# Projections of an attention layer in chunks of 512 columns instead of 256, with weights in three places and transposes dealt out one token tile behind

## The chip, the cores and the metric

The kernel runs on one core of one Trainium2 chip. The metric is the device time of one execution in microseconds (us), lower is better. The engines are named as in the profile: PE (TensorE, matrix products and transposes), PEld (its weight loads), DVE (VectorE), ACT (ScalarE), POOL (GpSimd) and SP (SyncE, which here only issues DMAs). They run at the same time, each its own instructions in order, and wait for each other by semaphores.

## The reference, cut to what matters

One inference step of a two-layer decoder. The first layer is a matrix LSTM, the second is attention with forget gates; each is followed by a SwiGLU feed-forward part. A prompt of 16 + 1024 tokens and a sample batch of 8 x 8 tokens use the same weights, so T = 1104 token rows are worked on. The change lies in the second mixer, in these projections (D = 1024, 16 heads of 64 columns):

```python
def shared_kv(h, g_kv, w_kvf, b_f, k_g):
    xs = rmsnorm(h, g_kv)
    p = xs @ w_kvf
    k = rmsnorm(p[..., :HD].reshape(B, T, H_B, DH_B), k_g)
    v = p[..., HD:2 * HD].reshape(B, T, H_B, DH_B)
    lf = jax.nn.log_sigmoid((p[..., 2 * HD:] + b_f).astype(jnp.float32))
...
    q = rmsnorm(p[..., :HD].reshape(B, T, H_B, DH_B), q_g) * DH_B ** -0.5
    og = p[..., HD:]
    o = attend(q, k, v, lf).reshape(B, T, HD)
    return (o * jax.nn.sigmoid(og)) @ w_out
```

Keys and queries are normalised per head and token row; keys, values and log-forget values are also outputs.

## The kernel before

**Precision.** Every product is made of three fp32r matmuls (`mm3`, L162 to L166): high part by high part, high by low, low by high. Activations and weights are split into a high part (ACT, with the gain of the norm: L228) and a low part (DVE, L229).

**Tokens.** There are nine token tiles `TT`, the first of 80 rows (64 sample, 16 prompt) and eight of 128. Three of them make a group (`GRP`, `TS`: 336, 384 and 384 tokens), held as activation tiles x0, x1 and x2, high and low (x0h, x0l and so on).

**The stage that changes** is the first part of `phase_b` (L1548). It makes the values, keys and queries for all tokens, in chunks of 256 columns: value chunks 3, 1 and 2 (number 3 first, with the 16 forget columns, 272 in all; value columns 0 to 255 were made earlier), then four key chunks and four query chunks. `tm_proj` (L277) does one chunk. It loads the weights as two halves of four blocks of 128 rows (`load_w`, L199: 512 KB each, issued by SP at L221), from ten places of [128, 1088] that were laid out before: two raw, four high, four low, taken in turn. Then for each of the nine token tiles it does 8 blocks x 3 = 24 matmuls into one PSUM bank (`tmps`, four of them), with the token tile as the loaded operand and the weights as the moving one. `evac` empties the bank.

- For values, `evac` is one copy on ACT into `vst`; the rows go out by POOL's DMA queue (`out_p_v` and the scratch `vD`, 1 MB each, L1543). After chunk 3 come `forget` (L1699: log-sigmoid on DVE; three groups of transposes `fgps` of the forget columns on PE through one PSUM place, each followed by a copy `ltB` on ACT, L1715; a scan on DVE, transposes `fgcq`), preparation for sample attention, and the loads of the first cache page.
- For keys and queries, `evac` (L1607) copies the bank into `raw` on ACT (L1608), squares it on ACT (L1610), and sums the squares per head on DVE (L1611). After every third token tile `then` (L1643) makes the norms of the group: square root on ACT (L1645), reciprocal on DVE (L1646), and the scaling of `raw` on DVE (128 x 768, L1648).
- `turn` (L1614) transposes a group, one feature block of 128 columns at a time: three PE transposes into `btp` (L1622, two PSUM places), the high part `bhi` on ACT (L1626), the low part `blo` on DVE (L1627, two places each), and POOL's DMA stores into the scratch `kDh`, `kDl`, `qDh`, `qDl` (L1631) and, in the first group, `kS` or `qS` (L1635) from `bst`. For keys POOL also multiplies `raw` by the norm's gain (L1637) and sends the rows out (`out_rows`, L1571). A group's `turn` is put on the list `behind` and is done when the next group's `then` comes, three tiles later.

**Behind the stage.** The output gate's first block is projected (`gate(0)`, L1655 to L1663, `og0ps`), and the last group's turn is done. Then sample attention begins (L1665). It loads the queries `qtS` back from the scratch (L1833), transposes cache pages (`ktp`, L1868, copied to `kT` at L1869) and makes scores (`sps`, L1877); the other gates' matmuls (`bps`) are dealt between. The weights of gate 7 have a place of their own, `w7`.

**What sets the order.** In `phase_b` up to the gate, the order on each engine is chosen by the framework's scheduler from the program order and what is free. In sample attention the order of PE is that of the program text. ACT, DVE and POOL run in the order in which the scheduler emitted them; an instruction that waits holds up all behind it on its engine.

Of the kernel before, what the change touches and what calls it, by code (L numbers as in the profile page):

```python
# [147 lines left out]
class Net:  # L148
# [50 lines left out]
    def load_w(self, pieces, g=None, nk=KT, keep=None):  # L199

        nc = self.nc
        n = sum(p.shape[1] for p in pieces)
        new = lambda pool, nm, dt, bufs: pool.tile([P, max(nk * n, self.wmin)], dt, name=self.uid(nm), tag=nm, bufs=bufs)[
            :, : nk * n].rearrange("p (k n) -> p k n", k=nk)
        if self.slots:

            x = self.slot
            cut = lambda t: t[:, : nk * n].rearrange("p (k n) -> p k n", k=nk)
            raw = cut(self.slots[x % 2])
            self.slot += 1  # L210
        else:
            raw = new(self.wp, "wraw", F32, self.wbufs[0])
        if self.slots and not keep:
            hi, lo = (cut(self.slots[y]) for y in (2 + x % 4, 6 + x % 4))
        else:
            pool, bufs = (keep, 1) if keep else (self.wp, self.wbufs[1])
            hi, lo = (new(pool, nm, F32R, bufs) for nm in ("whi", "wlo"))
        o = 0
        for p in pieces:
            w = p.shape[1]  # L220
            nc.sync.dma_start(raw[:, :, o : o + w], p.rearrange("(k p) n -> p k n", p=P))  # L221
            o += w
        if g is None:
            self.split(raw, hi, lo)
        else:
            for k in range(nk):
                gk = self.gain[:, g + k : g + k + 1]
                nc.scalar.activation(hi[:, k], raw[:, k], AF.Copy, scale=gk)  # L228
# [139 lines left out]
    def mlp(self, H, w, l, heads=None, cb=None):  # L368
# [3 lines left out]
        with self.pool(self.uid("nsp")) as sp, self.pool(self.uid("npp"), bufs=2, space=PSUM) as pn:  # L372
# [3 lines left out]
            if cb:  # L376
# [4 lines left out]
            slots = {x: wp.tile([P, max(self.wmin, KT * P)], F32 if x < 2 else F32R, name=self.uid("slot"))  # L381
                     for x in (range(10) if cb else (*range(2, 10), 0, 1))}
# [1165 lines left out]
def phase_b(self, ys, w7, cb):  # L1548
# [8 lines left out]
    self.lfD = scr("lfD", [NS, HB])  # L1557
    ck = ExitStack()
    sk = ck.enter_context(self.pool("spk"))
    with self.pool("fb", bufs=2) as fp, self.pool("fbp", bufs=2, space=PSUM) as pp:  # L1560
        gn = fp.tile([P, DH], F32, name="gk", bufs=1)
        nc.scalar.dma_start(gn, I["k_norm_b"].partition_broadcast(P))
        gc = fp.tile([P, 2], F32, name="gqk", bufs=1)
# [11 lines left out]
            nc.gpsimd.dma_start(po[NM:, cs].rearrange("(i p) d -> p i d", p=P), t[:, 1:, :])  # L1575

        flat = lambda a: a.rearrange("t h d -> t (h d)")

        for c in (3, 1, 2):
            vs = fp.tile([P, NT, 256], F32, name=f"vst{c}", tag="vst")  # L1580

            def evac(i, m, ps):
                nc.scalar.copy(vs[:m, i, :], ps[:m, :256])
                if c == 3:
                    nc.scalar.copy(lf[:m, i, :], ps[:m, 256:272])

            self.tm_proj([wkv[:, D + 256 * c : D + 256 * c + (272 if c == 3 else 256)]], G_KV, pp, "b", 4, evac)
            cs = slice(256 * c, 256 * c + 256)
            self.value_rows(vs, 0, cs)
            if c == 3:  # L1590
                self.forget(lf)
                cq, ncn = self.sample_prep(sk)
                masks = self.sample_masks(sk)
                self.page = {}
                self.load_page(sk, 0)


        behind = []
        for w, g, gi, dst, dstS in ((wkv, G_KV, 0, self.kD, self.kS), (wqo, G_B, 1, self.qD, self.qS)):
            gcol = gc[:, gi : gi + 1]  # L1600
            for c in range(4):
                raw = fp.tile([P, NT, 256], F32, name=self.uid("raw"), tag="raw")
                nc.gpsimd.memset(raw[NS:, 0, :], 0.0)
                ss = fp.tile([P, NT, 4], F32, name=self.uid("ss"), tag="ss")
                nc.gpsimd.memset(ss, 1.0)

                def evac(i, m, ps):  # L1607
                    nc.scalar.copy(raw[:m, i, :], ps[:m, :256])  # L1608
                    sq = fp.tile([P, 256], F32, name=self.uid("sqb"), tag="sqb")
                    nc.scalar.activation(sq[:m], ps[:m, :256], AF.Square)  # L1610
                    nc.vector.tensor_reduce(out=ss[:m, i, :], in_=sq[:m].rearrange("p (h d) -> p h d", d=DH),  # L1611
                                            op=ALU.add, axis=AX.X)

                def turn(q, v4, c=c, raw=raw, gi=gi, gcol=gcol, dst=dst, dstS=dstS):  # L1614
                    for hp in range(2):
                        f = 2 * c + hp
                        ps = pp.tile([P, 512], F32, name=self.uid("btp"), tag="bt")
                        g0, g1 = TS[q]
                        n = g1 - g0
                        for i in GRP[q]:  # L1620
                            t0, t1 = TT[i]
                            nc.tensor.transpose(ps[:, t0 - g0 : t1 - g0], raw[: t1 - t0, i, hp * P : hp * P + P],  # L1622
                                                self.ident[: t1 - t0, : t1 - t0])
                        hi = fp.tile([P, SL], F32R, name=self.uid("bhi"), tag="bhi")
                        lo = fp.tile([P, SL], F32R, name=self.uid("blo"), tag="blo")
                        nc.scalar.activation(hi[:, :n], ps[:, :n], AF.Copy, scale=gcol)  # L1626
                        nc.vector.scalar_tensor_tensor(out=lo[:, :n], in0=ps[:, :n], scalar=gcol,  # L1627
                                                       in1=hi[:, :n].bitcast(F32), op0=ALU.mult, op1=ALU.subtract)
                        o = max(NS - g0, 0)
                        for z, x in enumerate((hi, lo)):  # L1630
                            nc.gpsimd.dma_start(dst[z][f, :, g0 + o - NS : g1 - NS], x[:, o:n].bitcast(F32))  # L1631
                        if q == 0:
                            st = fp.tile([P, T0], F32, name=self.uid("bst"), tag="bst")
                            nc.vector.tensor_scalar(out=st, in0=ps[:, :T0], scalar1=gcol, scalar2=None, op0=ALU.mult)
                            nc.gpsimd.dma_start(dstS[f], st)  # L1635
                    if gi == 0:
                        nc.gpsimd.tensor_tensor(out=v4, in0=v4, in1=gn.unsqueeze(1).broadcast_to([P, 12, DH]),  # L1637
                                                op=ALU.mult)
                    if gi == 0 and q == 2:
                        out_rows(raw, flat(O["p_k"][0]), flat(O["s_k"].rearrange("b t h d -> (b t) h d")),  # L1640
                                 slice(256 * c, 256 * c + 256))

                def then(q, raw=raw, ss=ss, turn=turn):  # L1643
                    qs = slice(3 * q, 3 * q + 3)
                    nc.scalar.activation(ss[:, qs], ss[:, qs], AF.Sqrt, scale=1.0 / DH, bias=self.eps)  # L1645
                    nc.vector.reciprocal(ss[:, qs], ss[:, qs])  # L1646
                    v4 = raw[:, qs, :].rearrange("p i (h d) -> p (i h) d", d=DH)
                    nc.vector.tensor_tensor(out=v4, in0=v4, in1=ss[:, qs, :].rearrange(  # L1648
                        "p i h -> p (i h)").unsqueeze(2).broadcast_to([P, 12, DH]), op=ALU.mult)
                    if behind:  # L1650
                        behind.pop()()
                    behind.append(lambda: turn(q, v4))

                self.tm_proj([w[:, 256 * c : 256 * c + 256]], g, pp, "b", 4, evac, then)
# [715 lines left out]
```

## Time and profile before

| | |
|---|---|
| time, median of 3 runs | 2985.75 us (2976.2 to 2991.02) |
| profiled execution | 2988.03 us |
| its span (first to last instruction) | 2986.3 us |
| mean granted PE clock | 0.984 |
| value chunks 1 and 2, keys and queries | about 1430 to 1682 us |
| one key or query chunk | 27.02 us |

The stage is a twelfth of the span. A row of the timeline gives start, duration, engine, line, operation, output and inputs with shapes, and in brackets the idle time before it with what ended it. Durations of matmuls are modelled ends of a pipelined engine, so that they overlap; the distance from start to start is the pace. "x6" joins six instructions in a row. In a window's row, the columns are busy times of PE, PEld, DVE, ACT and POOL.

### The profile page before, as it was taken

The numbers are of one execution on the slowest core, as the hardware profiler recorded it, in microseconds if no ns is written. First come the engines' busy times: TensorE is split into PE (matmuls) and PEld (weight loads), VectorE is DVE, ScalarE is ACT, GpSimd is POOL, SyncE is SP. The second block draws the span as 40 slices with busy tenths as digits, with TensorE's granted clock in tenths as the row PEclk, the third lists the DMA queues.
The fourth block names the chain that finished last, engine by engine and source line by source line (L and its number), as shares of the span: only waits on it lengthen the run. The fifth ranks groups of instructions, "written<-read, shape, count | busy, mean of one in ns | idle before, by whom it ended". The sixth has DMA issues, their size and how long they took to land.

```text
span 2986.3 us, 52654 instructions
## 1 busy us (share of the span) xinstructions
PE 2881.3 (96%) x20974; PEld 2762.6 (93%) x20974; DVE 1430.3 (48%) x2864; ACT 1140.4 (38%) x2069; POOL 779.4 (26%) x1174
## 2 busy tenths in 40 slices
PE   7999997999999999999999999999999999999999
PEld 7998886999999999999999888777899999999998
DVE  5032456564444455554355543777464444445543
ACT  5122264232222234333344454777332222224432
POOL 2011223313232221104354201454232232231110
PEclk9999799999999999999999999999999999999999
DMA  7052445222222156454354576443413222216653
GB/s 222 7 136 82 114 113 170 94 82 90 72 66 87 54 197 214 155 193 143 128 168 148 196 271 230 159 170 103 139 54 110 74 66 87 71 65 230 210 183 104
DMA packets 298336, 392.73 MB, mean 132 GB/s; under 512 B 31790, under 2 KB 220234, under 8 KB 297066
## 3 DMA queue, kind: packets, MB, share of 16 engines
q1 hardware_dynamic: 260674, 266.90, 27.7%
q0 software_dynamic: 33744, 120.15, 12.2%
q8 instruction: 165, 2.70, 0.4%
q10 hardware_dynamic: 3672, 2.31, 0.3%
q14 instruction: 81, 0.66, 0.1%
HBM read 292.19 MB, written 97.10 MB: 130 GB/s over the span
## 4 chain that ended last, share of the span: by engine, by line
PE 76%; DVE 5%; ACT 3%; issue 3%; POOL 2%; DMA 1%; DVEq 0%; POOLq 0%; ACTq 0%
PE m L1193 21%; PE dps L164 6%; PE dps L166 6%; PE dps L165 6%; PE fps L166 4%; PE fps L164 4%; PE fps L165 4%; PE tmps L164 3%; PE tmps L165 3%; PE tmps L166 3%; PE sp L2157 1%; PE pops L166 1%; PE pops L165 1%; PE pops L164 1%; DVE s L2161 1%
## 5 line engine op out<-in xcount | busy, mean ns | idle before, releaser
L235 DVE TENSOR_TENSOR slot<-slot,slot 128x1024 fp32r<-128x1024 f32 x164 | 207.1, 1266 | 204.4 <-ACT slot L234 204.2
L234 ACT CAST slot<-slot 128x1024 fp32r<-128x1024 f32 x164 | 171.9, 1050 | 336.6 <-PE m L1193 103.3
L166 PE MATMUL fps<-x0h,slot 128*128 128x336 f32 x688 | 219.0, 318 | 1.4 <-DVE slot L235 1.4
L164 PE MATMUL fps<-x0h,slot 128*128 128x336 f32 x688 | 219.4, 319 | 0.1
L165 PE MATMUL fps<-x0l,slot 128*128 128x336 f32 x688 | 218.3, 317 | 0.0
L1193 PE MATMUL m<-x2h,slot 128*128 128x384 f32 x704 | 193.7, 336 | 0.0
L1193 PE MATMUL m<-x1h,slot 128*128 128x384 f32 x672 | 185.9, 338 | 0.0
L307 POOL TENSOR_TENSOR ns<-ns,nq 128x384 f32<-128x384 f32 (+1 forms) x72 | 77.1, 1071 | 278.2 <-ACT nq L305 276.9
L1290 POOL DMA_DIRECT2D hr<-hT x68 | 37.0, 544 | 395.4 <-DMA hT<-fs 84.1
L166 PEld LDWEIGHTS fps<-x0h,slot 128*128 128x128 f32 x688 | 129.8, 189 | 1.9 <-DVE slot L235 1.9
L164 PEld LDWEIGHTS fps<-x0h,slot 128*128 128x128 f32 x688 | 129.9, 189 | 1.3 <-ACT slot L234 0.7
L165 PEld LDWEIGHTS fps<-x0l,slot 128*128 128x128 f32 x688 | 130.1, 189 | 0.4 <-issue 0.3
L1193 PEld LDWEIGHTS m<-x2h,slot 128*128 128x128 f32 x704 | 128.5, 188 | 0.0
L1193 PEld LDWEIGHTS m<-x1h,slot 128*128 128x128 f32 x672 | 123.7, 190 | 0.0
L1193 PE MATMUL m<-x2l,slot 128*128 128x384 f32 x352 | 118.5, 337 | 0.1
L234 ACT CAST slot<-vA 128x1024 fp32r<-128x1024 f32 x53 | 55.5, 1050 | 156.7 <-PE m L1193 76.3
L234 ACT CAST slot<-Ht 128x1024 fp32r<-128x1024 f32 x53 | 55.5, 1049 | 156.1 <-PE m L1193 75.7
L1193 PE MATMUL m<-x1l,slot 128*128 128x384 f32 x336 | 113.4, 337 | 0.0
L235 DVE TENSOR_TENSOR slot<-vA,slot 128x1024 fp32r<-128x1024 f32 x53 | 66.8, 1262 | 85.4 <-ACT slot L234 85.3
L235 DVE TENSOR_TENSOR slot<-Ht,slot 128x1024 fp32r<-128x1024 f32 x53 | 66.9, 1264 | 85.0 <-ACT slot L234 84.9
L2184 ACT ACTIVATE s<-s,nb 128x272 f32<-128x272 f32 (+7 forms) x126 | 98.9, 787 | 0.0
L1193 PE MATMUL m<-T_4h,slot 128*128 128x384 f32 x352 | 97.7, 338 | 0.0
(757 smaller groups left out, 9335.4 us busy)
## 6 DMA issues: line engine op xcount, KB each, us to landing
slot<-in_w_down SPq DMA_DIRECT2D x88, 512.0 KB
fs<-in_w_down SPq DMA_DIRECT2D x44, 512.0 KB
hr<-hT POOLq DMA_DIRECT2D x46, 384.0 KB, 5.2
slot<-in_w_gate_up SPq DMA_DIRECT2D x32, 512.0 KB
kp<-in_cache_k SPq DMA_DIRECT2D x32, 512.0 KB
vp<-in_cache_v SPq DMA_DIRECT2D x32, 512.0 KB
vA<-in_w_gate_up SPq DMA_DIRECT2D x28, 512.0 KB
Ht<-in_w_gate_up SPq DMA_DIRECT2D x28, 512.0 KB
```

The source lines that it names most:

```text
L164: mm(ps, sh, mh, start=first, stop=False)
L165: mm(ps, sh, ml, start=False, stop=False)
L166: mm(ps, sl, mh, start=False, stop=last)
L234: self.nc.scalar.copy(hi, src)
L235: self.nc.vector.tensor_tensor(out=lo, in0=src, in1=hi.bitcast(F32), op=ALU.subtract)
L307: (nc.vector if x == KT - 1 else nc.gpsimd).tensor_tensor(out=s, in0=s, in1=sq, op=ALU.add)
L1193: nc.tensor.matmul(u.ps[b], w[p][:, k], x[q][:, k], start=first and k == i == 0, stop=k == 3 and i == 2, skip_group_check=True)
L1290: nc.gpsimd.dma_start(hraw[j], hT[t][:, 2 * c : 2 * c + 2])
L2157: nc.tensor.matmul(ps[z][:, :n], a[r, qs], b[r, at : at + n], start=(y == 0), stop=(y == 2))
L2161: nc.vector.tensor_tensor_reduce(out=ss[z, u][:, at + o : at + e], in0=ps[z][:, o:e], in1=diag[x][:, z] if y else ncb[:, z, at + o : at + ...
L2184: nc.scalar.activation(ss[z, u], ss[z, u], AF.Exp, bias=nb[:, z : z + 1], accum_out=sm[:, u, z : z + 1])
```

## The change

- **Chunks.** Value chunk 3 with the forget columns stays as it is. The rest is done in five chunks of 512 columns: one of values, two of keys, two of queries (`project`). A token tile is now 24 matmuls of 512 columns into one whole PSUM bank. `raw`, the squares, the sums, the scaling (128 x 1536) and POOL's product (128 x 1536) are twice as wide and half as many. `raw` and `vst` share two places of [128, 9, 512].
- **Weights.** A half chunk is 4 blocks x 512 columns (1 MB), loaded by `load_half`. All half chunks go through one raw place (the two old ones joined). The split parts lie in three places: two from the eight old ones, one in `w7t` (high) and `w3` (low). Half 2x + 2 is asked for at the start of chunk x, half 2x + 3 in its last token tile. The place of gate 7's weights, `w7t`, is therefore laid out ahead of the stage, and `load_w` takes `keep` as a pair of places.
- **Transposes.** A group now has four feature blocks. Each `turn` does one, and two are done behind each token tile's `evac`, from the next tile on: the first two one tile after `then`, the others two tiles after. The group left at the end does its four turns in a row behind gate 0 (before: two feature blocks).

The layouts and PE's instructions outside this stage are the same. The core of the diff:

```diff
@@ load_w
-        if self.slots and not keep:
-            hi, lo = (cut(self.slots[y]) for y in (2 + x % 4, 6 + x % 4))
+        if self.slots:
+            hi, lo = (cut(y) for y in keep or (self.slots[2 + x % 4], self.slots[6 + x % 4]))
...
@@ phase_b
+    w7t = w7.tile([P, 2 * self.wmin], F32R, name="w7t")
...
-        for c in (3, 1, 2):
-            vs = fp.tile([P, NT, 256], F32, name=f"vst{c}", tag="vst")
+        new = lambda nm: fp.tile([P, NT, 512], F32, name=nm, tag="rv")
+        vs = new("vst3")
...
+        self.tm_proj([wkv[:, D + 768 : D + 1040]], G_KV, pp, "b", 4, evac)
+        self.value_rows(vs[:, :, :256], 0, slice(768, 1024))
+        self.forget(lf)
...
+        f2 = cf.enter_context(self.pool("fb2", bufs=2))
+        w3 = f2.tile([P, 2048], F32R, name="w3", bufs=1)
+        n = 2 * self.wmin
+        parts = [(self.wide[1][:, y * n : y * n + n], self.wide[1][:, 2 * n + y * n : 3 * n + y * n])
+                 for y in (1, 0)] + [(w7t, w3)]
+        chunks = [(wkv, D + 256, G_KV)] + [(w, 512 * c, g) for w, g in ((wkv, G_KV), (wqo, G_B)) for c in range(2)]
+        ready = {}
+
+        def load_half(y):
+            if y >= 2 * len(chunks):
+                return
+            w, c0, g = chunks[y // 2]
+            view = lambda a: a[:, :2048].rearrange("p (k n) -> p k n", k=4)
+            raw = view(self.wide[0])
+            hi, lo = ready[y] = [view(a) for a in parts[y % 3]]
+            r0 = y % 2 * 512
+            nc.sync.dma_start(raw, w[r0 : r0 + 512, c0 : c0 + 512].rearrange("(k p) n -> p k n", p=P))
+            for k in range(4):
+                gk = self.gain[:, g + y % 2 * 4 + k : g + y % 2 * 4 + k + 1]
+                nc.scalar.activation(hi[:, k], raw[:, k], AF.Copy, scale=gk)
+                nc.vector.scalar_tensor_tensor(out=lo[:, k], in0=raw[:, k], scalar=gk, in1=hi[:, k].bitcast(F32),
+                                               op0=ALU.mult, op1=ALU.subtract)
+
+        behind = []
+
+        def project(x, evac, then=None):
+            if x == 0:
+                load_half(0)
+                load_half(1)
+            load_half(2 * x + 2)
+            for i, (t0, t1) in enumerate(TT):
+                m = t1 - t0
+                ps = pp.tile([P, 512], F32, name=self.uid("tmps"), tag="b", bufs=4)
+                for k in range(KT):
+                    wh, wl = ready[2 * x + k // 4]
+                    xh, xl = self.x_tile(i, k)
+                    self.mm3(ps[:m], xh, xl, wh[:, k % 4, :], wl[:, k % 4, :], k == 0, k == KT - 1)
+                if i == NT - 1:
+                    load_half(2 * x + 3)
+                evac(i, m, ps)
+                for _ in range(2):
+                    if behind:
+                        behind.pop(0)()
+                if then and i % 3 == 2:
+                    then(i // 3)
+
+        vs = new("vst1")
+        project(0, lambda i, m, ps: nc.scalar.copy(vs[:m, i, :], ps[:m]))
+        self.value_rows(vs, 0, slice(256, 768))
...
             def then(q, raw=raw, ss=ss, turn=turn):
...
-                    if behind:
-                        behind.pop()()
-                    behind.append(lambda: turn(q, v4))
+                behind.extend(lambda hp=hp: turn(q, hp, v4) for hp in range(4))
...
-        behind.pop()()
+        for x in behind:
+            x()
...
-                    self.w7 = gate(7, keep=w7)
+                    self.w7 = gate(7, keep=(w7t[:, : self.wmin], w7t[:, self.wmin :]))
```

More of the change, by code (lines that the diff above doesn't have):

```diff
@@ L212, in load_w @@
             raw = new(self.wp, "wraw", F32, self.wbufs[0])
-        if self.slots and not keep:
-            hi, lo = (cut(self.slots[y]) for y in (2 + x % 4, 6 + x % 4))
-        else:
-            pool, bufs = (keep, 1) if keep else (self.wp, self.wbufs[1])
-            hi, lo = (new(pool, nm, F32R, bufs) for nm in ("whi", "wlo"))
+        if self.slots:
+            hi, lo = (cut(y) for y in keep or (self.slots[2 + x % 4], self.slots[6 + x % 4]))
+        else:
+            hi, lo = (new(self.wp, nm, F32R, self.wbufs[1]) for nm in ("whi", "wlo"))
         o = 0
@@ L380, in mlp @@
             self.slot = 0
-            slots = {x: wp.tile([P, max(self.wmin, KT * P)], F32 if x < 2 else F32R, name=self.uid("slot"))
-                     for x in (range(10) if cb else (*range(2, 10), 0, 1))}
+            if cb:
+                n = self.wmin
+                self.wide = [wp.tile([P, y * n], dt, name=self.uid("wide")) for y, dt in ((2, F32), (8, F32R))]
+                slots = {x: self.wide[x > 1][:, (x - 2 * (x > 1)) * n : (x - 2 * (x > 1) + 1) * n] for x in range(10)}
+            else:
+                slots = {x: wp.tile([P, KT * P], F32 if x < 2 else F32R, name=self.uid("slot"))
+                         for x in (*range(2, 10), 0, 1)}
             with ExitStack() as c:
@@ L1559, in phase_b @@
     sk = ck.enter_context(self.pool("spk"))
-    with self.pool("fb", bufs=2) as fp, self.pool("fbp", bufs=2, space=PSUM) as pp:
+    w7t = w7.tile([P, 2 * self.wmin], F32R, name="w7t")
+    with self.pool("fb", bufs=2) as fp, self.pool("fbp", bufs=2, space=PSUM) as pp, ExitStack() as cf:
         gn = fp.tile([P, DH], F32, name="gk", bufs=1)
@@ L1577, in phase_b @@
         flat = lambda a: a.rearrange("t h d -> t (h d)")
-        for c in (3, 1, 2):
-            vs = fp.tile([P, NT, 256], F32, name=f"vst{c}", tag="vst")
-            def evac(i, m, ps):
[L1583 to L1595, printed above, removed]
@@ L1598, in phase_b @@
[L1598 to L1639, printed above, removed]
-                        out_rows(raw, flat(O["p_k"][0]), flat(O["s_k"].rearrange("b t h d -> (b t) h d")),
[L1641 to L1649, printed above, removed]
-                    if behind:
-                        behind.pop()()
-                    behind.append(lambda: turn(q, v4))
-                self.tm_proj([w[:, 256 * c : 256 * c + 256]], g, pp, "b", 4, evac, then)
@@ new lines, in phase_b, with evac @@
+        new = lambda nm: fp.tile([P, NT, 512], F32, name=nm, tag="rv")
+        vs = new("vst3")
+        def evac(i, m, ps):
+            nc.scalar.copy(vs[:m, i, :256], ps[:m, :256])
+            nc.scalar.copy(lf[:m, i, :], ps[:m, 256:272])
+        self.tm_proj([wkv[:, D + 768 : D + 1040]], G_KV, pp, "b", 4, evac)
+        self.value_rows(vs[:, :, :256], 0, slice(768, 1024))
+        self.forget(lf)
+        cq, ncn = self.sample_prep(sk)
+        masks = self.sample_masks(sk)
+        self.page = {}
@@ new lines, in phase_b @@
+        self.load_page(sk, 0)
+        f2 = cf.enter_context(self.pool("fb2", bufs=2))
[19 more added lines that the diff above has]
+                                               op0=ALU.mult, op1=ALU.subtract)
```

45 lines of the change are left out of this document (added).

## The prediction

> **What bounds the kernel now.** I read the head of the page first, then busy time by windows around the stage that changes, then single rows.
>
> ```profile
> span 2986.3 us, 52654 instructions
> ## 1 busy us (share of the span) xinstructions
> PE 2881.3 (96%) x20974; PEld 2762.6 (93%) x20974; DVE 1430.3 (48%) x2864; ACT 1140.4 (38%) x2069; POOL 779.4 (26%) x1174
> ```
>
> ```profile
> PE 76%; DVE 5%; ACT 3%; issue 3%; POOL 2%; DMA 1%; DVEq 0%; POOLq 0%; ACTq 0%
> ```
>
> PE is busy for 96% of the span and makes 76% of the chain that ended last, so a gain has to come from PE's own work or from one of its few gaps. Around the change (columns: window, length, busy time with instruction count for PE, PEld, DVE, ACT and POOL, granted clock, DMA share, GB/s):
>
> ```profile
> 1510.79:1645.90 135.11, 135.11 (x1173) 135.11 (x1172) 71.59 (x155) 61.61 (x175) 62.37 (x99) 1.00 0.46 149
> 1690.00:1720.00 30.00, 24.99 (x240) 21.40 (x244) 11.31 (x41) 10.91 (x21) 4.48 (x9) 0.94 0.91 312
> 1696.00:1698.00 2.00, 2.00 (x9) 2.00 (x9) 0.00 (x0) 0.00 (x0) 0.00 (x0) 0.50 1.04 360
> ```
>
> In the key and query chunks PE is busy without a gap at a granted clock of 1.00, while DVE and ACT stand at about half and DMA at 0.46. Idle time of PE lies at the edges: 5 us where sample attention starts (1690 to 1720, where the clock also fell to 0.50 for a while), and 1.5 us near the forget step (waits, below). So inside the stage nothing but PE's pace can give time, and any wait that reaches PE there is a loss.
>
> **The change, part by part.**
>
> *PE's work.* Ten 256-column chunks of 216 matmuls (2160) become five 512-column chunks of 216 (1080). The 144 transposes stay, the 272-column chunk stays, and outside this stage PE's instructions are the same. The question is the pace at 512 columns.
>
> ```profile
> 1483.77 0.74 PE L1622 MATMUL btp<-ident,raw 80*128 80x80 f32 x6
> ...
> 1510.79 0.74 PE L1622 MATMUL btp<-ident,raw 80*128 80x80 f32 x6
> ```
>
> ```profile
> 655.64 14.67 PE m L1193 x84
> ```
>
> ```profile
> 2067.68 0.40 PE L2157 MATMUL sp<-kl,qh 64*128 64x512 f32 x2
> 2067.90 0.40 PE L2157 MATMUL sp<-kh,ql 64*128 64x512 f32 x2
> 2068.13 0.21 PE L2239 MATMUL tp<-ident,rx 64*128 64x64 f32 x1
> ```
>
> One 256-column chunk takes 1510.79 - 1483.77 = 27.02 us. Its 18 transposes, as one run, hold PE about 1.6 us (the 0.74 us of six is a modelled end; the next matmul follows after about 0.5). That leaves 25.4/216 = 117.5 ns for a matmul, 0.459 ns per column. At 384 columns it is 14.67/84 = 174.6 ns (row of the chain), 0.455 per column. At 512 columns the only rows are the score matmuls with 64 rows, two side by side: 2067.90 - 2067.68 = 220 ns and 2068.13 - 2067.90 = 230 ns, 0.43 to 0.45. Time goes with columns; hardly any of it is a price per instruction. From 256 and 384 a straight line gives 174.6 + (174.6 - 117.5) = 231.7 at 512; I take 230, with 220 and 2 x 117.5 = 235 as ends. 1080 x 230 = 248.4, against about 252 now (a few of the value chunks run at 115): **-3.6 us**, ends -14 and +2.
>
> The Trainium skill, "TensorE: Matmul & The Clock Gate", section "Back-to-back issue gap", gives N/2.4 + 2.5 ns, an estimate of 215.8 ns at 512 columns and of 162.5 at 384. The trace's 174.6 at 384 disagrees, as it does with the 131 ns at 512 columns that the section gives as sustained; by the formula this term would be -19 us instead of -3.6.
>
> *Evacuation, squares, scaling.* Half as many instructions of double width on ACT, DVE and POOL; all have room. What decides is the chain that the transposes now wait for. Before, a group's transposes ran a whole group (three tiles) later; now the first two run one tile after it. Rows of a chain (copy, then root, then scaling):
>
> ```profile
> 1475.81 0.37 ACT L1608 COPY raw<-tmps 128x256 f32<-128x256 f32 x1 [2.18 <-PE tmps L166]
> ...
> 1477.00 1.28 ACT L1645 ACT_TABLE_LOAD   x1 [0.53 <-DVE ss L1611]
> ...
> 1478.89 0.96 DVE L1648 TENSOR_TENSOR raw<-raw,ss 128x768 f32<-128x768 f32 x1
> ```
>
> ```profile
> 1539.57 1.84 POOL L1637 TENSOR_TENSOR raw<-raw,gk 128x768 f32<-128x768 f32 x1
> ...
> 1540.37 1.86 DVE L1648 TENSOR_TENSOR raw<-raw,ss 128x768 f32<-128x768 f32 x1
> ```
>
> ```profile
> L1869 ACT COPY kT<-ktp x32: 564/588/591, 1698.7 to 1831.8; 128x512 f32<-128x512 f32 x32
> ```
>
> From the copy's start to the scaling's end is 1479.85 - 1475.81 = 4.04 us, less 1.28 of a table load that comes once: 2.8 us. A 512-column copy takes 588 ns where 256 take 370, a factor 1.6; doubled work everywhere is 2. So the new chain is 2.8 x 1.6 = 4.4 us, ends 2.8 and 5.6. The cover is one tile of 24 matmuls, 5.5 us, and one matmul more. I cost it at nothing, with 1 us to spare, except once with the table load (4.4 + 1.3 - 5.7): **+0.3 us**. If the cover is gone, each of 11 groups stalls PE (a rival below).
>
> *Weights.* A half chunk is now 1 MB into one raw place, where 512 KB went into two. The second half of the next chunk is split during the last tile of this one. The first half of the chunk after next can be sent for only then, and its split on ACT stands ahead of the next chunk's evacuations.
>
> ```profile
> 1682.75 9.69 SPq L221 DMA_DIRECT2D slot<-in_w_qo_b  x3
> ```
>
> ```profile
> 1686.89 0.70 ACT L228 ACTIVATE whi<-slot,gain 128x128 fp32r<-128x128 f32 x2 [0.55 <-DMA slot<-in_w_qo_b]
> ```
>
> 512 KB took 4.1 us from issue to the split that waited for it, so 1 MB takes 4.1 (all latency) to 8.3 us. ACT then waits in order until about 7 us into a chunk and comes to the first tile's copy after 9 to 10 instead of 5.5. PE goes on, since there are four PSUM places. What is late is the previous group's four turns, behind that copy in ACT and with two PSUM places of their own; three chunk changes at 0 to 2 us, taken as **+1 us** in all.
>
> *The forget step.* PE's waits in the stage, and the rows around it:
>
> ```profile
> PE ktp L1868 <- DVE kT L1869: 2.9, 2, 2.1
> PE sps L1877 <- DVE qb L1858: 1.6, 1, 1.6
> PE ktp L1868 <- DVE blo L1627: 1.4, 1, 1.4
> PE fgcq L1723 <- DVE cnB L1719: 1.0, 1, 1.0
> PE fgps L1714 <- DVE lfB L253: 0.5, 1, 0.5
> ```
>
> ```profile
> 1413.53 2.53 SPq L221 DMA_DIRECT2D slot<-in_w_kvf  x2
> ```
>
> ```profile
> 1424.45 0.44 ACT L1715 ACTIVATE ltB<-fgps 16x336 f32<-16x336 f32 x1 [1.70 <-PE fgps L1714]
> ```
>
> ```profile
> vD<-vst POOLq DMA_DIRECT2D x1, 1024.0 KB, 9.7
> ```
>
> After the change four splits of the third half chunk stand on ACT ahead of the 1424.45 copy, and the second of the three forget transposes waits for that copy. Their 1 MB can be sent for about 2 us after the 272-column chunk ends (1413.7), in the same time as this store of 1 MB and another like it. It lands between 6 us after 1413.7 (4.1 of transfer) and 15 (8.3, and half of a store's 9.7 beside it); I take 12, nearer to the upper end, since they run at the same time. Four splits of 0.6 us follow (588 ns for 512 columns, above), so the copy comes after 8 to 17 us, at 12 + 2.4 = 14.4 by my value, while PE wants it after almost two tiles of 5.5, at 11. That is a stall of 0 to 6, here 3.4, with the hand-over to PE and a piece at a lowered clock after a fresh gap some 1.5 more: **+5 us**, ends 0 and 8.
>
> *The end of the last chunk.*
>
> ```profile
> 1681.98 0.81 PE L1622 MATMUL btp<-ident,raw 128*128 128x128 f32 x6
> ...
> 1693.72 0.39 ACTq L1833 DMA_DIRECT2D qtS<-qS  x1
> ...
> 1700.39 0.64 PE L1877 MATMUL sps<-kT,qb 128*32 128x128 f32 x16 [1.58 <-DVE qb L1858]
> ```
>
> ```profile
> qDh<-bhi POOLq DMA_DIRECT2D x4, 192.0 KB, 3.7
> ```
>
> The last tile ends at 1681.98 and the first score matmul of sample attention starts 18.4 us later, after the queries' load (issued at +11.7, used 6.2 us after). Now the last group has four turns left and no tile behind which to hide them. Their two places of high and low parts are free only when a store of 3.7 us has landed, so the third and fourth turn each wait for one; between them stand the splits of gates 1, 2, 3 and 7, and the queries' load is issued behind gate 7's split (8 pieces) on ACT. By these rows it goes out at about +17.5 instead of +11.7, and the first score matmul follows at +24.3: 5.9 us late, and 1 us more at the half clock (0.50 in the window 1696 to 1698, after a gap of this kind). **+7 us**, ends 2 and 10.
>
> *Sum:* -3.6 + 0.3 + 1 + 5 + 7 = **+9.7 us**. The profiled execution took 2988.03 us (span 2986.3 and 1.7 around it), 2.3 above the median of 2985.75. So 2997.7 from the profiled run and 2995.5 from the median; I say 2997.
>
> **The rivals.**
>
> *Slower: the scaling chain is not covered.* Price: at the upper end, 5.6 us and 1.8 more where the scaling meets POOL's product (1540.37: 1.86 us where 0.96 is usual, beside the 1.84 of POOL's row), 7.4 against 5.7. With work of ACT and DVE in front it is about 2 us for each of 11 groups, 22 us. Beside the sum's other terms: 2988 + 9.7 + 22 = 3020. It decides from a chain of 5.7 us on. For it: every group has only one tile now, and the splits share the engines. Against it: factor 1.6 of the copy, and POOL's product lies after the fourth turn, mostly clear of the next scaling. Chance 0.30.
>
> *Faster: a lower price per column at 512.* If the 220 ns of the first score row are the true pace, or less (216), PE's term is -14 to -19; with the edges at their lower ends (2 us) 2988 - 19 + 2 = 2971, and 2968 at best. Against it: 174.6 at 384. Chance 0.17, and with it the time falls just beyond 0.5% faster.
>
> *It does little:* the edges hide in slack, PE's term alone counts: 2984. Chance 0.11.
>
> **How the numbers follow.** Forecast as summed (2988 to 3006): 0.42, of which 0.08 lies beyond 0.5%. A measurement of this kernel can tell about 0.5% (15 us) from no change. Slower 0.30 + 0.08 = 0.38; within 0.5% 0.34 + 0.11 = 0.45; faster 0.17. The range reaches from 2970 (most of the faster case) to 3022 (most of the slower one). The likeliest case's own range is 2988 to 3006, from the lower and upper ends of the two edge terms.
>
> **What would show it.** Right: matmuls of the 512-column chunks 230 ns apart; no wait of PE for the scaling inside a chunk beyond the first; a wait of the second forget transpose for ACT's copy of 3 to 5 us; the first score matmul some 24 us after the last tile; everything after 1720 only shifted. Wrong: 216 to 220 ns apart (faster by 10 us and more), a wait of 1 to 3 us before the first turn of every group (slower), or edges without new waits (no change).

## The result, and the profile after

The changed kernel takes 3004.94 us (median of 7 runs, 3002.79 to 3015.17) against 2979.03 us of the kernel before on the same chips (7 runs): a ratio of 1.0089, 95% interval 1.0070 to 1.0108, so 21 to 32 us slower. Its profiled execution took 3004.47 us.

The head of its page:

```profile
span 3002.8 us, 50151 instructions
## 1 busy us (share of the span) xinstructions
PE 2883.7 (96%) x19894; PEld 2709.5 (90%) x19894; DVE 1417.9 (47%) x2764; ACT 1127.3 (38%) x1936; POOL 772.3 (26%) x1148
```

1080 instructions of PE are gone, and its busy time is the same (2881.3 before). So fewer instructions bought nothing, and 16.5 us more of the span went to waits and to pace. Whole spans of single profiles mislead here, though: the changed kernel came 9.3 us earlier to the end of its 272-column chunk than the kernel before, in instructions that are the same (the last section tells why). I therefore measure from that point, the start of the last 272-column matmul (1413.6 us in the kernel before; the stage begins there and not at about 1430, as the table ahead of the prediction has it), to four others: the last matmul of the last chunk, the first and the last score matmul of sample attention (`sps`), and the first transpose of prompt attention (`tp`). Start to start, in us of the profiles (e1 to e10 are the experiments below):

| stretch | before | after | e1 | e2 | e5 | e7 | e9 | e10 |
|---|---|---|---|---|---|---|---|---|
| chunks of the stage | 268.3 | 272.5 | 272.6 | 268.8 | 267.1 | 267.1 | 267.1 | 267.1 |
| to the first score | 18.5 | 26.3 | 26.2 | 18.7 | 25.9 | 24.1 | 24.0 | 19.8 |
| sample attention | 133.6 | 134.5 | 134.7 | 135.2 | 136.4 | 134.6 | 134.1 | 135.0 |
| to prompt attention's first transpose | 43.6 | 53.3 | 43.5 | 55.1 | 53.1 | 44.9 | 44.9 | 43.5 |
| sum | 464.0 | 486.5 | 477.0 | 477.8 | 482.5 | 470.7 | 470.1 | 465.4 |

The changed kernel loses 22.6 us in this stretch: 4.3 in the chunks, 7.7 ahead of the first score, 0.9 in sample attention, 9.7 at the start of prompt attention, some 150 us behind the end of the stage. The 0.9 means little: that row goes from 133.6 to 136.4 in the table, between kernels with the same work there. From the last point to the end of the span it takes 3.1 us more than the kernel before, again in the same instructions; in the thirteen profiles that tail goes from 1106.8 to 1111.9 us.

**The pace.** PE's rows at the first turn of a key group, in two key chunks and one query chunk:

```profile
1485.42 0.39 PE L164 MATMUL tmps<-w7t,x1h 128*128 128x512 f32 x1
1485.65 0.75 PE L1676 MATMUL btp<-ident,raw 80*128 80x80 f32 x6
```

```profile
1539.14 0.53 PE L1676 MATMUL btp<-ident,raw 80*128 80x80 f32 x4
```

```profile
1646.93 0.46 PE L1676 MATMUL btp<-ident,raw 80*128 80x80 f32 x3
```

A chunk of 512 columns takes 1539.14 - 1485.65 = 53.49 us; the two after it take 53.9 each on average. Two chunks of 256 took 2 x 27.02 = 54.04. Less the 36 transposes (3.3 us), the 216 matmuls are 232 to 235 ns apart. Measured from start to start, without the transposes, it is 233.6 ns on average in the key and query chunks, against 117.1 in the kernel before: 0.3% less than twice as much.

```profile
1485.65:1539.14 53.49, 53.49 (x253) 42.90 (x251) 26.04 (x39) 21.25 (x41) 27.75 (x35) 1.00 0.41 139
```

In this window PE is busy without a gap at clock 1.00. Its weight loads are busy for 42.90 of 53.49 us, where they were busy all the time before (135.11 of 135.11), and the time for a column has hardly moved (0.456 ns, from 0.457): the loads had not been what limited PE.

**The waits of PE**, from the end of the 272-column chunk to sample attention, and then around the start of prompt attention:

```profile
PE btp L1676 <- DVE blo L1681: 5.3, 2, 3.8
PE fgps L1766 <- ACT ltB L1767: 3.8, 1, 3.8
PE ktp L1920 <- DVE kT L1921: 3.5, 2, 2.8
PE btp L1676 <- DVE raw L1701: 0.9, 1, 0.9
PE fgps L1766 <- DVE lfB L252: 0.2, 1, 0.2
```

```profile
PE sp L2209 <- issue: 3.7, 1, 3.7
PE sp L2209 <- DVE mxf L2213: 1.6, 1, 1.6
PE sp L2209 <- DMA ql<-qDl: 1.5, 1, 1.5
PE sp L2209 <- DMA kl<-kDl: 1.0, 1, 1.0
```

The kernel before had one wait of 0.4 us in the second window. SP's queue says what is late there (after, then before):

```profile
1845.46 0.36 SPq L2128 DMA_DIRECT2D qh<-qDh  x1
1860.83 0.32 SPq L2128 DMA_DIRECT2D kh<-kDh  x1
```

```profile
1841.82 0.36 SPq L2076 DMA_DIRECT2D qh<-qDh  x1
1842.23 0.42 SPq L2076 DMA_DIRECT2D kh<-kDh  x1
```

The first keys of prompt attention (`kh`) were asked for 0.4 us behind the queries (`qh`). Now they wait 15 us longer, until just behind this row:

```profile
1860.47 0.33 PE L166 MATMUL bps<-x2h,wide 128*128 128x384 f32 x1
```

It is the last gate matmul, and it reads its weights from `wide`, the tile of eight places that the change has made out of eight tiles. SP's own waits from 1840 to 1862 us name it as what the keys' load (L2128) waited for; the kernel before has no such wait there:

```profile
SPq L2128 <- PE bps L166: 14.9, 1, 14.9
```

So the keys' place must take over room that `wide` held. (The profile shows the wait, not the addresses.) Then PE runs at half clock for a while:

```profile
1864.00:1868.00 4.00, 1.00 (x6) 0.63 (x6) 0.00 (x0) 0.00 (x0) 0.00 (x0) 0.50 0.98 377
1868.00:1872.00 4.00, 3.81 (x12) 3.01 (x12) 0.00 (x0) 0.00 (x0) 0.00 (x0) 0.50 0.83 291
```

### The profile page after: what moved, and what is told of

The parts are those of the page before. It is cut to its first block, busy times and chain, and to the rows that moved or that the text cites. A ratio compares the mean times of both kernels' runs of the same rounds, so it can differ in the third digit from the quotient of the medians.

```text
span 3002.8 us, 50151 instructions
## 1 busy us (share of the span) xinstructions
PE 2883.7 (96%) x19894; PEld 2709.5 (90%) x19894; DVE 1417.9 (47%) x2764; ACT 1127.3 (38%) x1936; POOL 772.3 (26%) x1148
## 5 line engine op out<-in xcount | busy, mean ns | idle before, releaser
L234 DVE TENSOR_TENSOR slot<-slot,slot 128x1024 fp32r<-128x1024 f32 x82 | 105.7, 1293 | 99.2 <-ACT slot L233 98.8
L234 DVE TENSOR_TENSOR wide<-wide,wide 128x1024 fp32r<-128x1024 f32 x82 | 101.4, 1240 | 102.2 <-ACT wide L233 102.2
L166 PE MATMUL fps<-x0h,slot 128*128 128x336 f32 x344 | 109.6, 319 | 0.7 <-DVE slot L234 0.7
L166 PE MATMUL fps<-x0h,wide 128*128 128x336 f32 x344 | 109.4, 318 | 0.7 <-DVE wide L234 0.7
L164 PE MATMUL fps<-x0h,wide 128*128 128x336 f32 x344 | 110.0, 320 | 0.0
L164 PE MATMUL fps<-x0h,slot 128*128 128x336 f32 x344 | 109.5, 318 | 0.1
L165 PE MATMUL fps<-x0l,wide 128*128 128x336 f32 x344 | 109.1, 317 | 0.0
L165 PE MATMUL fps<-x0l,slot 128*128 128x336 f32 x344 | 109.1, 317 | 0.0
L1198 PE MATMUL m<-x2h,slot 128*128 128x384 f32 x352 | 96.9, 336 | 0.0
L1198 PE MATMUL m<-x2h,wide 128*128 128x384 f32 x352 | 96.8, 336 | 0.0
L1198 PE MATMUL m<-x1h,slot 128*128 128x384 f32 x336 | 92.9, 338 | 0.0
L1198 PE MATMUL m<-x1h,wide 128*128 128x384 f32 x336 | 92.3, 335 | 0.0
```

What stands on the lines that cost most here:

```text
L164: mm(ps, sh, mh, start=first, stop=False)
L165: mm(ps, sh, ml, start=False, stop=False)
L166: mm(ps, sl, mh, start=False, stop=last)
L234: self.nc.vector.tensor_tensor(out=lo, in0=src, in1=hi.bitcast(F32), op=ALU.subtract)
L1198: nc.tensor.matmul(u.ps[b], w[p][:, k], x[q][:, k], start=first and k == i == 0, stop=k == 3 and i == 2, skip_group_check=True)
```

## The experiments

**Is it the joined tile? (e1 and e2)** One kernel undoes that part of the change, the other makes that part alone. First, the changed kernel with eight tiles; a half chunk's four blocks lie two by two in two of them:

```diff
-                self.wide = [wp.tile([P, y * n], dt, name=self.uid("wide")) for y, dt in ((2, F32), (8, F32R))]
-                slots = {x: self.wide[x > 1][:, ...] for x in range(10)}
+                self.wide = [wp.tile([P, 2 * n], F32, name=self.uid("wide"))]
+                slots = {x: self.wide[0][:, x * n : x * n + n] if x < 2 else wp.tile([P, n], F32R, name=self.uid("slot"))
+                         for x in range(10)}
...
+        two = lambda u, v: [a[:, k * 512 : k * 512 + 512] for a in (u, v) for k in range(2)]
```

> The changed kernel with its eight old split places kept as eight tiles (a half chunk uses two of each kind); the raw place stays joined. Theory A (the joined tile of 8 places is given back only as a whole, so the first key load of prompt attention waits for the last gate matmul): the load goes out right behind the query load, about 1845 us instead of 1861, the 3.7 + 1.0 + 1.5 us of PE's waits at the first scores are gone, the stretch from the first scores to the first tp transposes is 20 us as in the kernel before instead of 26; about 10 to 11 us faster than the changed kernel, so +12 to +16 us over the kernel before. Rival (the key and query scratch is written later, or the DMA queue is busy): no change there.

Measured: ratio 1.0042 (1.0025 to 1.0058), 11 runs, 12.2 us over the kernel before, as the theory had it. The keys go out at once, and the last row of the table's column is the kernel before again (43.5 against 43.6):

```profile
1842.90 0.35 SPq L2130 DMA_DIRECT2D qh<-qDh  x1
1843.31 0.42 SPq L2130 DMA_DIRECT2D kh<-kDh  x1
```

Second, the kernel before with its ten places cut out of two tiles and nothing else:

```diff
-            slots = {x: wp.tile([P, max(self.wmin, KT * P)], F32 if x < 2 else F32R, name=self.uid("slot"))
-                     for x in (range(10) if cb else (*range(2, 10), 0, 1))}
+            if cb:
+                n = self.wmin
+                self.wide = [wp.tile([P, y * n], dt, name=self.uid("wide")) for y, dt in ((2, F32), (8, F32R))]
+                slots = {x: self.wide[x > 1][:, (x - 2 * (x > 1)) * n : (x - 2 * (x > 1) + 1) * n] for x in range(10)}
```

> The kernel before with nothing changed but that its eight split places are one tile and its two raw places another. Theory A: 9 to 11 us slower than the kernel before, all of it between 1845 and 1880 us, with waits of PE for the first key loads. Rival (the delay belongs to the chunks of 512): equal to the kernel before within 3 us.

Measured: 1.0039 (1.0025 to 1.0052), 12 runs, 11.6 us, and 11.5 us in the last row of the table.

```profile
1840.65 0.36 SPq L2081 DMA_DIRECT2D qh<-qDh  x1
1856.01 0.32 SPq L2081 DMA_DIRECT2D kh<-kDh  x1
```

SP's wait for the last gate matmul is back as well (1836 to 1860 us):

```profile
SPq L2081 <- PE bps L166: 14.9, 1, 14.9
```

The joined tile alone costs about 10 us, with chunks of 256 as with chunks of 512. Nothing in the stage itself shows it.

**The forget step (e3 and e5).** The changed kernel's ACT row and PE row there:

```profile
1416.80 2.56 ACT L1621 ACTIVATE w7t<-wide,gain 128x512 fp32r<-128x512 f32 x4 [6.04 <-DMA wide<-in_w_kvf]
1419.27 0.42 ACT L1767 ACTIVATE ltB<-fgps 16x336 f32<-16x336 f32 x1
```

```profile
1419.75 0.81 PE L1766 MATMUL fgps<-ident,lfB 128*16 128x128 f32 x3 [3.78 <-ACT ltB L1767]
```

ACT sits 6.04 us for the 1 MB and does four splits; only then comes the copy for which PE waits. PE stands still until 1419.75 us and then works at half clock to the end of this window:

```profile
1418.00:1424.80 6.80, 5.05 (x15) 3.73 (x16) 1.77 (x1) 3.24 (x7) 2.58 (x5) 0.50 0.10 10
```

(e3 to e6 were executed once each; they are read from their profiles alone.) First try:

```diff
-            load_half(2 * x + 2)
+            if x:
+                load_half(2 * x + 2)
             for i, (t0, t1) in enumerate(TT):
+                if x == 0 and i == 3:
+                    load_half(2)
```

> The changed kernel with the third half chunk asked for ahead of token tile 3 of the value chunk instead of ahead of tile 0. Theory (ACT's splits of that half stand in front of the forget copy): PE's wait for the forget copy falls from 3.8 us to under 0.7, and the end of the stage comes 3 to 4 us earlier against its start. Rival (the forget chain itself is late): the wait stays at 3 us or more.

Measured: the wait is still there, 4.1 us.

```profile
PE fgps L1769 <- ACT ltB L1770: 4.1, 1, 4.1
```

It settles nothing: in e3's timeline the load was issued 2.3 us behind the 272-column chunk as in the changed kernel, and ACT's splits still stand ahead of the copy. The scheduler orders by what is free, and the text three tiles later did not hold it. The second try gives the load something to wait for:

```diff
+            if x == 0:
+                nc.vector.tensor_copy(self.wide[0][:, :1], self.cqP[:, 0, :1])
             load_half(2 * x + 2)
```

> The changed kernel with the third half chunk's load made to wait for the forget step: one extra copy of a column of the forget step's result into the raw place ahead of the load (the column is overwritten by the load). On ACT the three forget copies now stand ahead of the splits. Theory: PE's wait for the forget copy (3.8 to 4.1 us so far) is gone, under 0.5; the wait for the scan comes back at about 1 us as in the kernel before; no half clock behind it; the stage from the end of the 272-column chunk to its last matmul falls from 272.5 to 267 to 269 us. Rival (the forget chain itself is late at this pace): a wait of 3 us or more stays.

Measured (waits of PE in the stage, all of them):

```profile
PE fgcq L1777 <- DVE cnB L1773: 0.8, 1, 0.8
PE fgps L1768 <- DVE lfB L252: 0.2, 1, 0.2
```

The wait is gone, so is the half clock behind it, and the stage takes 267.1 us, 5.4 less than in the changed kernel and 1.1 less than before. The theory holds. This is also the cleanest figure for the chunks of 512: with no new wait left in the stage they are worth at most 1.1 us. Of these 0.5 are shorter waits (0.8 + 0.2 here, 1.0 + 0.5 in the kernel before), so the wider matmuls themselves give some 0.6.

**The end of the last chunk (e4, e6, e8, e9, e10).** The first score comes 7.7 us late. The rows of ACT, and DVE's last low part:

```profile
1687.54 0.58 ACT L1680 ACTIVATE bhi<-btp,gqk 128x384 fp32r<-128x384 f32 x1 [1.91 <-DMA og2D<-og0s]
```

```profile
1694.90 0.62 DVE L1681 SCALAR_TENSOR_TENSOR blo<-btp,gqk,bhi 128x384 fp32r<-128x384 f32 x1 [3.18 <-DMA qDl<-blo]
```

```profile
1695.55 0.39 ACTq L1885 DMA_DIRECT2D qtS<-qS  x1
```

High and low parts wait for stores to land (gate 0's result uses a high part's place too), and the queries' load goes out behind the last of them, 18.7 us after the last tile. So, more places (`bhi` four, `blo` three, in the pool that is opened behind the forget step):

```diff
-                hi = fp.tile([P, SL], F32R, name=self.uid("bhi"), tag="bhi")
-                lo = fp.tile([P, SL], F32R, name=self.uid("blo"), tag="blo")
+                hi = f2.tile([P, SL], F32R, name=self.uid("bhi"), tag="bhi", bufs=4)
+                lo = f2.tile([P, SL], F32R, name=self.uid("blo"), tag="blo", bufs=3)
```

> The changed kernel with four places for the high parts (and gate 0) and three for the low parts of the transposes instead of two each. Theory (the last four turns wait for stores to land): PE's wait for blo falls from 5.3 us to under 2.5, and the first score matmul of sample attention comes 3 to 6 us earlier against the end of the last tile (26 us now). Rival (the splits of gates 1, 2, 3 and 7 in front on ACT and DVE set the end): the first score comes at most 2 us earlier.

Measured: the wait for `blo` falls from 5.3 to 1.5 us, the queries' load goes out at +14.9, and the first score at +24.3, only 2.0 earlier, which is the rival's figure. The wait moved on to the page copies:

```profile
PE ktp L1920 <- DVE kT L1921: 7.4, 2, 4.1
PE btp L1676 <- DVE blo L1681: 1.5, 1, 1.5
```

Are the two additional turns to blame at all?

```diff
-        for x in behind:
-            x()
+        for x in behind[:2]:
+            x()
```

> The changed kernel without the transposes and splits of the last two feature blocks of the last query group; their stores are kept, but store the first two blocks' parts again, so the queries of four heads are not the reference's. Theory (the end is late because four turns are left where two were): the first score matmul comes 18 to 20 us behind the last tile's end instead of 26.2 (the kernel before: 18.5). Rival (the splits of gates 1, 2, 3 and 7 set the end): 23 us or more.

Measured: the first score at +25.7. With only two turns left the end is as late as with four, so my reading of the end ("four turns are left where two were") is wrong as it stands. Here too the wait moved on: ACT waited 3.6 us for gate 7's weights ahead of the queries' load (+17.6), and PE's last wait before the first score was 3.7 us for the queries.

The three mends together, and then the same with queries ahead of keys:

> Eight separate split places, the third half behind the forget step, and four and three places for the parts of the transposes, together. From the single runs: the prompt start gives back 9.7, the forget step 4 to 5, the end 2 of the 22.6 us that the changed kernel lost. Theory: 5 to 7 us slower than the kernel before, 0.2%; the matmuls of 512 columns give nothing. Rival (512 columns do give 3.6 us or more once the waits are gone): equal to the kernel before or faster.

Measured: 1.0014 (1.0000 to 1.0029), 12 runs, so 0 to 9 us slower; the sum of the stretch 470.7, 6.7 above the kernel before. The rival that 512 columns give 3.6 us or more falls by the stage itself, which is 1.1 us shorter than before with its waits gone.

```diff
-for w, g in ((wkv, G_KV), (wqo, G_B)) for c in range(2)]
+for w, g in ((wqo, G_B), (wkv, G_KV)) for c in range(2)]
```

> As e7_three_mended, with the two query chunks ahead of the two key chunks, so that the queries' load for sample attention waits for no turn of the last chunk. Theory (the end is set by the queries' round trip through memory behind the last turns): the first score matmul comes 2 us or more earlier than in e7_three_mended (24.3 us behind the last tile). Rival (ACT's and DVE's order of turns and gate splits sets it, whatever is transposed last, and the keys add their rows' stores): no earlier, or later.

Measured: 1.0062 (1.0043 to 1.0081), 6 runs, and the first score at +31.5, later by 7.4. PE waited 12.2 us for a page copy behind five loads of gate weights and their splits. ACT's rows:

```profile
1701.36 0.40 ACT L227 ACTIVATE w7t<-wide,gain 128x128 fp32r<-128x128 f32 x1 [7.19 <-DMA wide<-in_w_qo_b]
1701.46 0.39 ACTq L1889 DMA_DIRECT2D qtS<-qS  x1
```

The queries' load stands on ACT behind a wait of 7.19 us for gate 7's weights and goes out at +22.3, later than in e7 (+15.0) by 7.3. So the edit did not bring the queries earlier, although no turn held them any more, and this run decides nothing on their round trip; it shows that the order on ACT can hold their load as well as the turns can. (The profile doesn't show which part of the 7.4 the keys' row stores and POOL's product have.)

Next, four places for the low parts too, and gate 0's result out of the high parts' places:

> As e7_three_mended, with four places each for the high and the low parts, and gate 0's result in the place of the squares, so that none of the last four turns waits for a store to land. Theory (the end is late because the last turns wait for places whose stores are under way): no wait of ACT or DVE for a store between the last tile and the queries' load, the load goes out 10.5 to 12.5 us behind the last tile (18.7 in the changed kernel, 15.0 in e7_three_mended, 11.9 before), the first score matmul 17 to 20 us behind it (26.2, 24.1, 18.5); in time within 0.15% of the kernel before, on either side, since the 512 columns alone give 1 us. Rival (two more feature blocks cost their own work on ACT and DVE at the end): the first score at 22 us or more.

Measured: no store is waited for any more and the queries' load goes out at +9.9, 2 us earlier than in the kernel before. The first score stays at +24.0. In time this kernel is at 1.0004 (0.9990 to 1.0018), 12 runs. Half of my expectation of the stretch came in, and the number that mattered did not:

```profile
PE ktp L1924 <- DVE kT L1925: 7.2, 1, 7.2
```

```profile
1679.31 0.69 DVE L1925 COPY kT<-ktp 128x512 f32<-128x512 f32 x1 [1.03 <-PE ktp L1924]
1686.43 1.09 DVE L1914 COPY qb<-qtS 64x32 f32<-64x32 f32 x8 [6.44 <-DMA qtS<-qS]
1687.56 0.17 DVE L2047 COPY qmt<-qtS 64x16 f32<-64x16 f32 x1
1687.64 0.68 DVE L1925 COPY kT<-ktp 128x512 f32<-128x512 f32 x1
```

DVE's rows in order: the page's second copy (1687.64) stands behind the small copies out of the queries (`qb`), and these wait 6.44 us for the queries to land. In the kernel before, both page copies stood ahead of them. So the small copies go to POOL, in this kernel and, as a control, in the kernel before:

```diff
-                nc.vector.tensor_copy(Q[r, u::2, c : c + NQ], qt[r, u::2, b * NQ : (b + 1) * NQ])
+                (nc.vector if b > 1 else nc.gpsimd).tensor_copy(Q[r, u::2, c : c + NQ], qt[r, u::2, b * NQ : (b + 1) * NQ])
```

> As e9_four_places, with the small copies out of the loaded queries (first two batches, and the first block for the first 16 tokens) on POOL instead of DVE. In e9_four_places the queries' load went out at +9.9 us and PE's 7.2 us wait was for a page copy on DVE that stands behind these copies. Theory (the order on DVE, not the turns, is what is left of the late end): the 7.2 us wait is gone, the first score matmul comes 1 to 2.5 us behind the landing of the queries, 19 to 22 us behind the last tile (24.0 in e9_four_places, 18.5 before), and the kernel is at or below the kernel before, by 0 to 4 us. Rival (the queries' landing at +19 and what competes with it set the end): 23 us or more.

> Control: the kernel before with the same small copies on POOL. There the page copies stand ahead of the small ones already, so it should do nothing: the first score 18.5 to 20 us behind the last tile, time within 0.1% of the kernel before. Rival (the small copies are a cost by themselves): 2 to 4 us faster.

Measured: the first score at +19.8, 4.2 earlier, and the 7.2 us wait is gone. In its place PE waits for the queries themselves:

```profile
PE sps L1933 <- POOL qb L1914: 5.0, 1, 5.0
```

The ratio is 1.0005 (0.9993 to 1.0018), 12 runs: the kernel before, and no better. Time doesn't tell this kernel from e9's (1.0004); the 4.2 us are seen in the profile alone. The control is 0.9998 (0.9984 to 1.0011) with the first score at +19.1: there the same edit does nothing. With the tile divided, the half chunk held back, four places and the order on DVE mended, the loss of 22.6 us is down to 1.5 in the profile and to nothing that can be told in time. (1.5 is less than a single profile can tell: the control's stretch sums to 467.0, 3.0 more than that of the kernel before.) What the copies on POOL do without the other mends was not tried. A version that beats both kernels did not come of it.

## Why the prediction was right and wrong

The sign of the sum was right (+9.7 us), its size was not (+21 to +32), and the outcome that it called likeliest, within 0.5%, did not come. The time of 3004.94 us lies inside the range of 2988 to 3006 that went with the sum, but in part by luck: a loss with no term in the sum (the last step below) filled the upper part of that range. By its own steps:

- **PE's work, -3.6 us:** right in kind, too large. The matmuls came 233.6 ns apart where I took 230, close to the upper end that I had named, 2 x 117.5. 1080 x 233.6 against 2160 x 117.1 is -0.6 us, and stage against stage it is -1.1 with shorter waits (e5). The rival of a lower price per column is out.
- **The scaling chain, covered:** right. One chain inside a chunk, ACT's copy and DVE's scaling:

```profile
1551.60 0.59 ACT L1663 COPY raw<-tmps 128x512 f32<-128x512 f32 x1 [4.18 <-PE tmps L166]
```

```profile
1554.13 1.76 DVE L1701 TENSOR_TENSOR raw<-raw,ss 128x1536 f32<-128x1536 f32 x1
```

  It takes 1555.89 - 1551.60 = 4.3 us where I had 4.4, and PE waited for it once, 0.9 us, where no tile follows. (The +0.3 of this term was added wrongly: 4.4 + 1.3 - 5.7 is 0.) The rival that made the kernel slower by 22 us this way did not happen; it is slower for another reason.
- **Weights at the chunk changes, +1 us:** no wait of PE there.
- **The forget step, +5 us:** right in mechanism, shown by e5. It cost 5.4 us (272.5 to 267.1), with a wait of 3.8 where I had 3.4 and 5 us at half clock behind it, some 2.5 us lost where I had 1.5 with the hand-over.
- **The end of the last chunk, +7 us:** right in size (7.7), and only in part in its mechanism. I put it on four turns with two places, and on gate 7's splits. The waits for places were there as I had said, but more places gave 2.0 us (e4) and then 0.1 (e9 over e7), with no wait for a store left; e6 took two turns away and gained 0.6. Behind these waits stood the order in which the scheduler had put gate splits, page copies and copies out of the queries on ACT and DVE: mending it on DVE, with the places mended already, gave 4.2 (e10), and PE then waits for the queries themselves. Some 1.2 us are left, and the shares belong to this order of mends. That the scheduler's order depends on the number of turns is likely, but it isn't shown.
- **"Everything after 1720 only shifted": the step that failed.** I compared what the instructions outside the stage are and where their tiles lie, found no difference, and priced them at nothing. I did not compare what they wait for. Merging eight tiles into one changed no address and no instruction, but it changed when the place is given back, and the load that moves in next waited for the last reader of any of the eight. That is 9.7 us in the changed kernel, 11.6 us in time when made alone (e2). The forecast had no term and no rival for it. Without it the sum would have come out at 12.9 us against the 9.7 that I gave.

## What to carry to other kernels

When a change merges buffers, or cuts several out of one, follow each of them to the tile that takes its place later, however far behind, and compare the waits of every load, not only instructions and addresses. Wider matmuls save instructions; look at two widths in the trace first, and if the time goes with columns, expect little from them, and count the risk of larger loads and longer queues. Where a wait is taken away and the end doesn't move, read the in-order queue of the engine that is waited for next; the wait had company.

## What the hardware showed beyond that

The clock stays down for quite different times after one and the same short gap. Ahead of the chunk products of the first layer (`cs`) PE waits 2.2 us in both kernels, in the same instructions, and falls to half clock. A window of the kernel before and one of the changed kernel:

```profile
296.10:326.80 30.70, 30.70 (x94) 24.07 (x94) 11.00 (x29) 3.16 (x4) 1.08 (x2) 0.50 0.28 75
```

```profile
291.60:301.90 10.30, 10.30 (x33) 8.07 (x31) 3.57 (x10) 0.34 (x1) 0.00 (x0) 0.50 0.06 15
```

In one the clock was at 0.50 for 30.7 us, with PE busy all the while; in the other for 10.2, with PE just as busy. Of the thirteen profiles here four show the long form (the kernel before, e2, e8 and e11) and nine the short one. That is some 10 us of a span, as much as most effects in this study, and the reason why stretches and not spans are compared above. What decides between the two isn't shown, but something goes with it: in the four long ones the clock had been at half once already, for 3.4 us, some 14 us before, behind a gap of 1.9 us that left it at 1.00 in the nine others. Two windows behind that gap, before and after the change:

```profile
281.10:286.10 5.00, 4.97 (x26) 4.93 (x27) 0.86 (x5) 0.37 (x1) 0.00 (x0) 0.66 0.38 105
```

```profile
279.80:284.80 5.00, 4.96 (x36) 4.92 (x37) 0.86 (x5) 0.37 (x1) 0.00 (x0) 1.00 0.38 105
```

The Trainium skill, "TensorE: Matmul & The Clock Gate", part "The HAM clock gate", says that only about the first 3.4 us of sustained work run at half clock. Neither form here fits that: at a PE that is busy without a gap the short one is three times as long, the long one nine times.
